# Casting weights layer by layer, and dilated attention by pairs of heads, in a four-layer decoder trunk on eight cores

## The chip, the cores and the metric

One Trainium2 chip, all eight of its cores. Each core takes two of the sixteen sequences of 4096 tokens through all four layers; the cores exchange nothing. The metric is the device time of the slowest core for one execution, in microseconds (us). Cores 0 to 3 are one die, 4 to 7 the other. Some executions are *slow*: the cores of one die, or of both, were granted a lower TensorE clock for part of the time, and the whole is some per cent longer.

Engines in the profile: PE is the TensorE matmul, PEld its weight load, DVE VectorE, ACT ScalarE, POOL GpSimd, SPq the queue on which the DMAs are issued. L763 is a line of the kernel in question.

## The reference, cut to what matters

Each layer normalises its input and projects it once (1024 to 6152 columns). It then runs two groups of heads on the result, projects their gated outputs back, and adds the input.

```python
def hybrid_layer(x, norm_g, w_in, ..., w_out):
    h = rms_norm(x, norm_g)
    proj = jnp.einsum('bsd,dn->bsn', h, w_in)            # stage A (and the gate columns, B)
    mq, mk, mv, mo, mz, mi, mf, aq, ak, av, az = jnp.split(proj, split_points, axis=-1)
    hm = mlstm_chunkwise(...)                            # stage C: 4 heads, recurrence by chunks of 64
    ...
    for window, dilation in ((128, 1), (512, 4), (2048, 16)):     # stage D: 8 heads of 64
        o, lse = dilated_window_attention(qa, ka, va, window, dilation)
    ...                                                  # outputs of the three patterns merged by lse
    y = jnp.einsum('bsm,md->bsd', jnp.concatenate([hm, ha], axis=-1), w_out)     # stage E
    return x + y
```

Attention cuts each residue class of the tokens into blocks of 128. A block of queries sees its own block of keys and the one before it. The first block of a class has no previous one. At dilation 16 a class has only 256 tokens, so every second block is a first one.

The weights come as float32 and the kernel multiplies in bfloat16, so every weight is read, scaled by norm_g where it belongs to the first projection, cast, and written back to memory once: "the weight cast".

Of the kernel before, what the change touches and what calls it, by code (L numbers as in the profile page):

```python
# [134 lines left out]
def build_program(S_TOK, NSEQ, DEPTH, debug=False):  # L135
# [24 lines left out]
    c_mask = din("c_mask", [128, 256], BF16)  # L160
# [27 lines left out]
    with ExitStack() as top:  # L188
# [14 lines left out]
        maskt = sbt(top, "maskt", [128, 256], BF16)  # L203
# [10 lines left out]

        def prologue():
            with ExitStack() as es:
                ng = sbt(es, "pl_ng", [128, DEPTH, 8], F32)
                for l in range(DEPTH):
                    S.dma('sp', ng[:, l, :], normg[l], writes=["pl_ng"])
                stg = Rot([(sbt(es, "pl_stg%d" % i, [128, 2048], F32), "pl_stg%d" % i) for i in range(3)])  # L220
                obf = Rot([(sbt(es, "pl_obf%d" % i, [128, 2048], BF16), "pl_obf%d" % i) for i in range(3)])
                engs = ['dve', 'act']
                k = 0
                for l in range(DEPTH):
                    for kc in range(8):
                        rows = slice(kc * 128, (kc + 1) * 128)
                        gcol = ng[:, l, kc:kc + 1]
                        pieces = [(w_in[l, rows, 0:2048], ws_in[l, :, kc * 6144:kc * 6144 + 2048], 2048),
                                  (w_in[l, rows, 2048:4096], ws_in[l, :, kc * 6144 + 2048:kc * 6144 + 4096], 2048),
                                  (w_in[l, rows, 4104:6152], ws_in[l, :, kc * 6144 + 4096:kc * 6144 + 6144], 2048),  # L230
                                  (w_g[l, rows, :], ws_g[l, :, kc * 256:(kc + 1) * 256], 256)]
                        for (src, dst, n) in pieces:
                            st, stk = stg.next()
                            ob, obk = obf.next()
                            S.dma('sp', st[:, 0:n], src, writes=[stk])
                            eng = engs[k % 2]
                            k += 1
                            if eng == 'act':
                                S.op('act', lambda e: e.activation(out=ob[:, 0:n], in_=st[:, 0:n], func=AF.Copy, scale=gcol),
                                     reads=[stk, "pl_ng"], writes=[obk])  # L240
                            else:
                                S.op(eng, lambda e: e.tensor_scalar(out=ob[:, 0:n], in0=st[:, 0:n], scalar1=gcol, scalar2=None, op0=ALU.mult),
                                     reads=[stk, "pl_ng"], writes=[obk])
                            S.dma('sp', dst, ob[:, 0:n], reads=[obk])
                    for mc in range(12):
                        st, stk = stg.next()
                        ob, obk = obf.next()
                        S.dma('sp', st[:, 0:1024], w_out[l, mc * 128:(mc + 1) * 128, :], writes=[stk])
                        eng = engs[k % 2]
                        k += 1  # L250
                        if eng == 'act':
                            S.op('act', lambda e: e.copy(out=ob[:, 0:1024], in_=st[:, 0:1024]), reads=[stk], writes=[obk])
                        else:
                            S.op(eng, lambda e: e.tensor_copy(out=ob[:, 0:1024], in_=st[:, 0:1024]), reads=[stk], writes=[obk])
                        S.dma('sp', ws_out[l, :, mc * 1024:(mc + 1) * 1024], ob[:, 0:1024], reads=[obk])
                S.barrier()
# [395 lines left out]
        def phase_D(l, s):  # L652
            t0 = s * S_TOK
            with ExitStack() as es:
# [5 lines left out]
                pex = Rot([(sbt(es, "D_pe%d" % i, [128, 256], BF16), "D_pe%d" % i) for i in range(4)])  # L660
                pmk = Rot([(sbt(es, "D_pm%d" % i, [128, 256], BF16), "D_pm%d" % i) for i in range(4)])
                ostg = Rot([(sbt(es, "D_os%d" % i, [128, 8, 65], F32), "D_os%d" % i) for i in range(3)])
                ps_s = Rot([(pst(es, "D_pss%d" % i, [128, 512], F32), "D_pss%d" % i) for i in range(4)])
                ps_o = Rot([(pst(es, "D_pso%d" % i, [128, 512], F32), "D_pso%d" % i) for i in range(4)])
# [32 lines left out]
                for pi, d in enumerate(PATTERNS):  # L697
# [4 lines left out]
                    for r in range(d):  # L702
                        for nb in range(nbd):
                            for h in range(8):
                                units.append((r, nb, h))
                    pending = []
                    state = {"po": None}
# [5 lines left out]
                    def emit_qk(u):  # L713
                        r, nb, h = u
                        qt, kt = QT[h // 2], KT[h // 2]
                        p0 = (h % 2) * 64
                        pss, pssk = ps_s.next()
                        W = 256 if nb > 0 else 128
                        S.op('pe', lambda e: e.matmul(pss[:, 0:128], lhsT=kt[p0:p0 + 64, tok(r, nb)], rhs=qt[p0:p0 + 64, tok(r, nb)], start=True, stop=True),  # L719
                             reads=[("KT", h // 2), ("QT", h // 2)], writes=[pssk], signal=(nb == 0))  # L720
                        if nb > 0:
                            S.op('pe', lambda e: e.matmul(pss[:, 128:256], lhsT=kt[p0:p0 + 64, tok(r, nb - 1)], rhs=qt[p0:p0 + 64, tok(r, nb)], start=True, stop=True),  # L722
                                 reads=[("KT", h // 2), ("QT", h // 2)], writes=[pssk])
                        px, pxk = pex.next()
                        S.op('act', lambda e: e.activation(out=px[:, 0:W], in_=pss[:, 0:W], func=AF.Exp, scale=0.125), reads=[pssk], writes=[pxk])  # L725
                        pm, pmk_ = pmk.next()
                        S.op('dve', lambda e: e.tensor_tensor(out=pm[:, 0:W], in0=px[:, 0:W], in1=maskt[:, 0:W], op=ALU.mult), reads=[pxk, "maskt"], writes=[pmk_])  # L727
                        pending.append((u, pm, pmk_))

                    def emit_pv():  # L730
                        (u, pm, pmk_) = pending.pop(0)
                        r, nb, h = u
                        b = r * nbd + nb
                        if h % 4 == 0:
                            state["po"] = ps_o.next()
                        po, pok = state["po"]
                        hs = (h % 4) * 65
                        S.op('pe', lambda e: e.matmul(po[:, hs:hs + 65], lhsT=pm[:, 0:128], rhs=V[:, b, h, 0:65], start=True, stop=(nb == 0)),  # L738
                             reads=[pmk_, (Vk, (b // 8) * 8), (Vk, "ones")], writes=[pok], signal=(nb == 0))
                        if nb > 0:  # L740
                            S.op('pe', lambda e: e.matmul(po[:, hs:hs + 65], lhsT=pm[:, 128:256], rhs=V[:, b - 1, h, 0:65], start=False, stop=True),  # L741
                                 reads=[pmk_, (Vk, ((b - 1) // 8) * 8), (Vk, "ones")], writes=[pok])
# [167 lines left out]
```

## The kernel before: the parts that the change touches

All engines are driven through one helper. `S.op(engine, ..., reads=[names], writes=[names])` and `S.dma('sp', out, in, reads, writes)` turn names of tiles into semaphores: an instruction waits for the last writers of what it reads, and for the last readers and writers of what it writes. `Rot([...]).next()` hands out a row of buffers in turn. There is one DMA queue, and it issues in program order.

The prologue casts all four layers ahead of everything else, one piece after the other:

```python
stg = Rot([... 3 buffers]);  obf = Rot([... 3 buffers])
for l in range(DEPTH):                       # 44 pieces a layer, 176 in all
    for (src, dst, n) in pieces:
        st, stk = stg.next();  ob, obk = obf.next()
        S.dma('sp', st[:, 0:n], src, writes=[stk])              # load
        ... cast on DVE or ACT in turn, st -> ob
        S.dma('sp', dst, ob[:, 0:n], reads=[obk])               # store: the queue waits here for the cast
```

Attention works on one head at a time. Two heads of 64 share a tile of 128 partitions: the even head is on partitions 0 to 63, the odd one on 64 to 127.

```python
ps_s = Rot([... 4 banks]);  ps_o = Rot([... 4 banks])
def emit_qk(u):
    r, nb, h = u
    p0 = (h % 2) * 64
    matmul(pss[:, 0:128],   lhsT=kt[p0:p0+64, tok(r, nb)],   rhs=qt[p0:p0+64, tok(r, nb)])      # L719, "score"
    if nb > 0:
        matmul(pss[:, 128:256], lhsT=kt[p0:p0+64, tok(r, nb-1)], rhs=qt[p0:p0+64, tok(r, nb)])  # L722, "score"
    activation(px[:, 0:W], pss[:, 0:W], Exp)                                                # ACT
    tensor_tensor(pm[:, 0:W], px[:, 0:W], maskt[:, 0:W], mult)                                # DVE
def emit_pv():                                # three units later
    matmul(po[:, hs:hs+65], lhsT=pm[:, 0:128],   rhs=V[:, b, h, 0:65])                         # L738, "value"
    if nb > 0:
        matmul(po[:, hs:hs+65], lhsT=pm[:, 128:256], rhs=V[:, b-1, h, 0:65])                   # L741, "value"
    ...  # every fourth head: copy po out on DVE or ACT; every eighth: store
for ui, u in enumerate(units):
    emit_qk(u)
    if len(pending) > 3: emit_pv()
    if ui == len(units) // 2: nextV = load_V(next dilation)     # fetch and cast the values of the next pattern
```

A score multiplies over 64 rows, a value over 128: the tensor engine changes its tiling between them, twice for each head.

## Time and profile before

20619.81 us, median of three runs (20401.18 to 20717.54).

Sums by stage, each the mean of the eight cores in the profiled execution, in us:

| stage | times | sum | each |
|---|---|---|---|
| weight cast | 1 | 1166 | |
| A projection | 8 | 7762 | 891 to 1010 |
| B gates | 8 | 647 | 81 |
| C recurrence | 8 | 2896 | 362 |
| D attention | 8 | 4463 | 557.9 |
| E output projection | 8 | 3649 | 456.1 |

The weight cast is counted from its first load, some 3.5 us after the start of the span. The spread in A goes with the clock: a projection that was granted 0.78 of full speed took some 1005 us, one that was granted 0.93 some 893. The lines of the profile stand in the prediction.

### The profile page before, as it was taken

How to read it: one execution, taken by the hardware profiler on the slowest of the kernel's cores; microseconds unless marked ns; L12 is line 12 of the kernel's file. 1: busy time of each engine (PE TensorE's matmuls, PEld its weight loads, DVE VectorE, ACT ScalarE, POOL GpSimd, SP SyncE). 2: the span in 40 equal slices, each digit the busy share in tenths (PEclk: the TensorE clock that was granted, in tenths of full speed). 3: DMA queues.
4: the chain of work that ended last, by engine and by line, in shares of the span. 5: the costliest groups of instructions: out<-in, count | busy, mean ns of one | idle time of the engine just before them, and what ended most of it. 6: DMA issues, size and time to landing. Idle time of an engine off the chain costs nothing.

```text
span 20716.2 us, 272538 instructions; the slowest of 8 cores (20382.5 to 20716.2 us)
## 1 busy us (share of the span) xinstructions
PE 13746.5 (66%) x64640; PEld 6212.6 (30%) x64640; DVE 7589.5 (37%) x17544; ACT 7610.3 (37%) x17513; POOL 1010.3 (5%) x1084
## 2 busy tenths in 40 slices
PE   0059376883869657695667928597476965779376
PEld 0023232332323223232323314233232322334232
DVE  0023542335423353234432354233542345323542
ACT  0034351434514353243513435143542435324451
POOL 0000000000000000000000000000000000000000
PEclk9997556875578656776568755787557765678657
DMA  4431225313242233423233131522324223332324
GB/s 166 166 129 70 98 87 151 105 69 122 85 161 75 81 108 111 138 73 97 92 136 114 71 118 69 179 78 71 118 96 150 77 83 106 117 132 75 100 88 151
DMA packets 1331733, 2233.47 MB, mean 108 GB/s; under 512 B 108304, under 2 KB 739344, under 8 KB 1306640
## 3 DMA queue, kind: packets, MB, share of 16 engines
q1 hardware_dynamic: 1330192, 2216.04, 31.3%
q8 instruction: 587, 9.62, 0.2%
q14 instruction: 954, 7.82, 0.1%
HBM read 1308.49 MB, written 907.15 MB: 107 GB/s over the span
## 4 chain that ended last, share of the span: by engine, by line
PE 58%; ACT 11%; DMA 10%; DVE 10%; issue 6%; SPq 2%; POOL 2%; DVEq 0%; ACTq 0%; POOLq 0%
PE A_pm_u L337 19%; PE E_py_u L827 9%; PE A_pm_u L330 9%; PE D_pss_u L719 7%; PE D_pso_u L738 5%; DMA D_Vstg_u<-s_av 3%; PE D_pss_u L722 3%; DMA pl_stg_u<-w_in 3%; ACT C_sqj_u L643 3%; SPq L108 2%; DVE C_t_u L639 1%; POOL E_ga_u L811 1%; ACT C_kw_u L609 1%; ACT A_sqj_u L300 1%; PE C_pso_u L623 1%
## 5 line engine op out<-in xcount | busy, mean ns | idle before, releaser
L337 PE MATMUL A_pm_u<-A_Wb_u,A_hT_u 128*128 128x512 bf16 x16384 | 4262.4, 425 | 0.0
L725 ACT ACTIVATE D_pe_u<-D_pss_u 128x256 bf16<-128x256 f32 (+1 forms) x6144 | 2200.1, 362 | 1228.4 <-ACT D_pe_u L725 455.9
L337 PEld LDWEIGHTS A_pm_u<-A_Wb_u,A_hT_u 128*128 128x128 bf16 x16384 | 1746.6, 107 | 2388.4 <-issue 1990.7
L727 DVE TENSOR_TENSOR D_pm_u<-D_pe_u,maskt_u 128x256 bf16<-128x256 bf16 (+1 forms) x6144 | 1692.8, 277 | 1911.5 <-PE D_pso_u L741 771.4
L330 PE MATMUL A_pm_u<-A_hT_u,A_Wb_u 128*128 128x512 bf16 x8192 | 2347.3, 440 | 0.0
L719 PE MATMUL D_pss_u<-D_Q_u,D_K_u 64*128 64x128 bf16 x6144 | 2044.9, 335 | 220.2 <-DMA D_K_u<-s_akT 218.8
L827 PE MATMUL E_py_u<-E_Wo_u,E_gT_u 128*128 128x512 bf16 x6144 | 1887.8, 479 | 174.4 <-DVE E_gT_u L822 174.4
L738 PE MATMUL D_pso_u<-D_V_u,D_pm_u 128*128 128x65 bf16 x6144 | 1450.2, 236 | 732.8 <-DVE D_pm_u L727 730.9
L722 PE MATMUL D_pss_u<-D_Q_u,D_K_u 64*128 64x128 bf16 x4800 | 1560.1, 325 | 0.0
L817 ACT COPY E_gT_u<-E_ptr_u 128x1024 bf16<-128x1024 bf16 x256 | 259.2, 1013 | 3291.4 <-PE E_ptr_u L815 3272.1
L738 PEld LDWEIGHTS D_pso_u<-D_V_u,D_pm_u 128*128 128x128 bf16 x6144 | 645.4, 105 | 2121.7 <-issue 2092.7
L330 PEld LDWEIGHTS A_pm_u<-A_hT_u,A_Wb_u 128*128 128x128 bf16 x8192 | 894.5, 110 | 1200.1 <-issue 1003.4
L358 DVE SCALAR_TENSOR_TENSOR A_acc_u<-A_cbuf_u,A_cw_u,A_acc_u 128x512 f32<-128x512 f32 x1536 | 1153.9, 751 | 164.5 <-DVE A_acc_u L358 3.2
L315 PE MATMUL A_ptr_u<-identb_u,A_xn_u 128*128 128x128 bf16 x2048 | 204.4, 260 | 1508.6 <-DMA A_xt_u<-x 1201.1
L741 PE MATMUL D_pso_u<-D_V_u,D_pm_u 128*128 128x65 bf16 x4800 | 1165.1, 243 | 0.0
L827 PEld LDWEIGHTS E_py_u<-E_Wo_u,E_gT_u 128*128 128x128 bf16 x6144 | 700.9, 117 | 1300.9 <-issue 957.4
L623 PE MATMUL C_pso_u<-C_Cb_u,C_q_u 128*128 128x257 bf16 x1024 | 420.2, 410 | 972.5 <-ACT C_Cb_u L612 972.5
L829 DVE TENSOR_TENSOR E_xo_u<-E_xt_u,E_py_u 128x512 f32<-128x512 f32 x512 | 352.1, 688 | 1778.5 <-PE E_py_u L827 1772.0
L621 PE MATMUL C_pso_u<-C_v_u,C_ST_u 128*128 128x257 bf16 x1024 | 411.9, 402 | 826.6 <-DVE C_ST_u L605 733.3
L643 ACT ACTIVATE C_sqj_u<-C_t_u 128x256 bf16<-128x256 f32 x1024 | 427.2, 417 | 1414.6 <-DVE C_t_u L639 1332.5
L355 DVE TENSOR_SCALAR A_acc_u<-A_cbuf_u,A_cw_u 128x512 f32<-128x512 f32 x512 | 249.2, 487 | 1884.8 <-ACT A_cbuf_u L354 1884.8
L719 PEld LDWEIGHTS D_pss_u<-D_Q_u,D_K_u 64*128 64x128 bf16 x6144 | 715.4, 117 | 744.3 <-issue 225.6
(98 smaller groups left out, 14543.5 us busy)
## 6 DMA issues: line engine op xcount, KB each, us to landing
s_od<-D_os_u SPq DMA_DIRECT2D x768, 260.0 KB, 2.1
E_o_u<-s_od SPq DMA_DIRECT2D x256, 780.0 KB, 6.9
pl_stg_u<-w_in SPq DMA_DIRECT2D x96, 1024.0 KB, 5.5
A_Wb_u<-ws_in SPq DMA_DIRECT2D x96, 1024.0 KB, 12.7
xs<-E_xo_u SPq DMA_DIRECT2D x192, 512.0 KB, 3.0
A_xt_u<-xs SPq DMA_DIRECT2D x192, 512.0 KB, 5.4
E_xt_u<-xs SPq DMA_DIRECT2D x192, 512.0 KB, 5.0
s_o<-A_tmo_u SPq DMA_DIRECT2D x256, 256.0 KB, 2.0
```

The source lines that it names most:

```text
L330: S.op('pe', lambda e: e.matmul(ps[:], lhsT=wtile[:, kc, col0:col0 + 128], rhs=hTt[:, kc, :], start=(kc == 0), stop=(kc == 7)), reads=[hk] ...
L337: S.op('pe', lambda e: e.matmul(ps[:], lhsT=hTt[:, kc, j * 128:(j + 1) * 128], rhs=Wb[:, kc, col0:col0 + 512], start=(kc == 0), stop=(kc = ...
L358: S.op('dve', lambda e: e.scalar_tensor_tensor(out=a[:], in0=cbuf[:, c, jt:jt + 512], scalar=cw[:, c, jt:jt + 1], in1=a[:], op0=ALU.mult, ...
L623: S.op('pe', lambda e: e.matmul(ps_o[:, h, 0:257], lhsT=q[:, h, ts], rhs=Cb[:, h, 0:257], start=False, stop=True), reads=[qk_, ("Cb", h)], ...
L643: S.op('act', lambda e: e.activation(out=sqj[:], in_=t1[:, h, :], func=AF.Square, accum_out=smt[:, 8 + h:9 + h]), reads=[(t1k, h)], writes ...
L719: S.op('pe', lambda e: e.matmul(pss[:, 0:128], lhsT=kt[p0:p0 + 64, tok(r, nb)], rhs=qt[p0:p0 + 64, tok(r, nb)], start=True, stop=True), re ...
L722: S.op('pe', lambda e: e.matmul(pss[:, 128:256], lhsT=kt[p0:p0 + 64, tok(r, nb - 1)], rhs=qt[p0:p0 + 64, tok(r, nb)], start=True, stop=Tru ...
L725: S.op('act', lambda e: e.activation(out=px[:, 0:W], in_=pss[:, 0:W], func=AF.Exp, scale=0.125), reads=[pssk], writes=[pxk])
L727: S.op('dve', lambda e: e.tensor_tensor(out=pm[:, 0:W], in0=px[:, 0:W], in1=maskt[:, 0:W], op=ALU.mult), reads=[pxk, "maskt"], writes=[pmk_])
L738: S.op('pe', lambda e: e.matmul(po[:, hs:hs + 65], lhsT=pm[:, 0:128], rhs=V[:, b, h, 0:65], start=True, stop=(nb == 0)), reads=[pmk_, (Vk, ...
L741: S.op('pe', lambda e: e.matmul(po[:, hs:hs + 65], lhsT=pm[:, 128:256], rhs=V[:, b - 1, h, 0:65], start=False, stop=True), reads=[pmk_, (V ...
L827: S.op('pe', lambda e: e.matmul(pyt[:], lhsT=gTt[:, mc, :], rhs=Wo[:, mc, half * 512:(half + 1) * 512], start=(mc == 0), stop=(mc == 11)), ...
```

## The change

Its intent is threefold. (1) Only layer 0's weights are cast in the prologue, with six staging and four output buffers, and five loads in flight: load k+5 is issued ahead of store k. (2) The 132 pieces of layers 1 to 3 are loaded, cast (on ACT) and stored in the output projection of the layer before, one for each 128-token tile, 22 in each of the first six of those stages. (3) Attention works on pairs of heads: the score matmuls alternate between the two row halves and write to two PSUM banks; one exponential and one mask multiplication serve both heads; then come the pair's values.

```diff
 prologue:
-for l in range(DEPTH): ... load; cast; store
+cst = Caster(es, 0, "pl")              # 6 staging buffers, 4 output buffers
+pcs = weight_pieces(0)
+lds = [cst.load(p) for p in pcs[:5]]
+for k in range(len(pcs)):
+    c = cst.cast(lds.pop(0), 'dve' if k % 2 == 0 else 'act')
+    if k + 5 < len(pcs):
+        lds.append(cst.load(pcs[k + 5]))
+    cst.store(c)

 phase_D:
-ps_s: 4 x [128, 512]     ps_o: 4 x [128, 512]
+ps_s: 3 x [128, 2, 512]  ps_o: 2 x [128, 512]    mask4 = maskt[:, 256:768]
 def emit_qk(u):
-    r, nb, h = u ... two matmuls of one head
+    r, nb, p = u
+    for w in range(nw):                       # own block, previous block
+        for a in range(2):                    # even head, odd head
+            ro = slice(a * 64, a * 64 + 64)
+            matmul(pss[:, a, w*128:(w+1)*128], lhsT=KT[p][ro, tok(r, nb - w)], rhs=QT[p][ro, tok(r, nb)])
+    activation(px[:, 0:W] as (a, w, i), pss[:, :, 0:128*nw], Exp)        # 512 columns
+    tensor_tensor(pm[:, 0:W], px[:, 0:W], mask4[:, 0:W], mult)
 def emit_pv():
+    for a in range(2):  ... the one or two value matmuls of head 2p + a
     ...

 phase_E, for each tile:
+    after the first transposes' copy:  if loaded: casted.append(cst.cast(loaded.pop(0)))      # ACT
+    after the tile's output store:     if casted: cst.store(casted.pop(0))
+                                       if jobs:   loaded.append(cst.load(jobs.pop(0)))
```

(Cut: the class `Caster`, the order of the pieces, the wider mask constant, and the split of the output staging's name in two.)

## The prediction

> **What bounds the kernel now.** I read in this order: the table of cores, the page, busy times by stage, then the timeline inside the stages that the change edits. The profiled run counts as slow (20717.54 us, 1.6% above the fastest of three at 20401.18), so I take the stages' inner structure from it and not its absolute level.
>
> The page:
>
> ```profile
> PE 13746.5 (66%) x64640; PEld 6212.6 (30%) x64640; DVE 7589.5 (37%) x17544; ACT 7610.3 (37%) x17513; POOL 1010.3 (5%) x1084
> PEclk9997556875578656776568755787557765678657
> ```
>
> Matmul time leads but there is no engine at its limit over the whole span; the clock row moves between 0.5 and 0.9, so the program is a row of stages with different limits. Busy times by stage (core 5: window and length, then PE, weight load, DVE, ACT, POOL, then clock, DMA share, GB/s). The lines are: weight cast, then projection, gates, recurrence, attention, output projection of the first sequence, then three stretches inside attention.
>
> ```profile
> 0.00:1181.27 1181.27, 0.00 (x0) 0.00 (x0) 98.95 (x88) 106.74 (x89) 0.20 (x4) 1.00 0.48 165
> 1181.27:2158.07 976.80, 861.10 (x3520) 365.36 (x3520) 299.83 (x432) 411.27 (x695) 80.38 (x97) 0.84 0.25 88
> 2158.07:2243.16 85.09, 6.59 (x32) 6.14 (x32) 34.84 (x16) 12.37 (x5) 0.10 (x1) 0.51 0.13 51
> 2243.16:2608.12 364.96, 118.51 (x640) 76.26 (x640) 227.35 (x640) 165.64 (x576) 7.91 (x3) 0.56 0.36 116
> 2608.12:3170.79 562.67, 447.96 (x2736) 209.20 (x2736) 245.78 (x870) 315.95 (x870) 1.04 (x2) 0.50 0.24 84
> 3170.79:3624.33 453.54, 269.07 (x1152) 116.12 (x1152) 128.27 (x224) 32.41 (x32) 36.85 (x32) 0.73 0.56 166
> 2614.00:2641.00 27.00, 0.58 (x4) 0.27 (x4) 1.23 (x1) 0.00 (x0) 0.00 (x0) 0.50 0.96 341
> 2726.00:2742.00 16.00, 0.00 (x0) 0.00 (x0) 2.45 (x2) 5.71 (x2) 0.00 (x0) 0.50 0.65 213
> 2886.00:2923.00 37.00, 0.00 (x0) 0.00 (x0) 2.45 (x2) 6.79 (x2) 0.00 (x0) 0.50 0.34 103
> ```
>
> The first 1181 us hold no matmul, and DMA is only half used: a serial chain. The five stages after it come eight times (four layers, two sequences); attention costs about 558 us each time, 4466 in all. In attention PE is busy 80% at half clock, apart from three stretches of 27, 16 and 37 us in which everything waits for loads.
>
> Why the weight cast is serial (timeline; start, length, what):
>
> ```profile
> 506.19 0.38 SPq L108 DMA_DIRECT2D pl_stg_u<-w_in  x1
> 511.45 1.29 DVE L242 TENSOR_SCALAR pl_obf_u<-pl_stg_u,pl_ng_u 128x2048 bf16<-128x2048 f32 x1 [10.68 <-DMA pl_stg_u<-w_in]
> 512.87 0.33 SPq L108 DMA_DIRECT2D ws_in<-pl_obf_u  x1
> 513.29 0.38 SPq L108 DMA_DIRECT2D pl_stg_u<-w_in  x1
> ```
>
> The next load is issued only after the previous piece's store, because the one queue waits for the cast before that store: one load in flight, though there are three buffers. 513.29 - 506.19 = 7.1 us for a 1 MB piece.
>
> What sets attention's pace (timeline, PE): a full head of dilation 1 or 4, the start of the next, then a full head of dilation 16 and, last, two lone first matmuls of the whole stage.
>
> ```profile
> 2930.35 0.29 PE L719 MATMUL D_pss_u<-D_Q_u,D_K_u 64*128 64x128 bf16 x1
> 2930.46 0.29 PE L722 MATMUL D_pss_u<-D_Q_u,D_K_u 64*128 64x128 bf16 x1
> 2930.68 0.24 PE L738 MATMUL D_pso_u<-D_V_u,D_pm_u 128*128 128x65 bf16 x1
> 2930.73 0.24 PE L741 MATMUL D_pso_u<-D_V_u,D_pm_u 128*128 128x65 bf16 x1
> 2930.91 0.29 PE L719 MATMUL D_pss_u<-D_Q_u,D_K_u 64*128 64x128 bf16 x1
> ```
> ```profile
> 2997.43 0.43 PE L719 MATMUL D_pss_u<-D_Q_u,D_K_u 64*128 64x128 bf16 x1
> 2997.68 0.41 PE L722 MATMUL D_pss_u<-D_Q_u,D_K_u 64*128 64x128 bf16 x1
> 2998.02 0.24 PE L738 MATMUL D_pso_u<-D_V_u,D_pm_u 128*128 128x65 bf16 x1
> 2998.19 0.43 PE L719 MATMUL D_pss_u<-D_Q_u,D_K_u 64*128 64x128 bf16 x1
> ```
> ```profile
> 2617.91 0.29 PE L719 MATMUL D_pss_u<-D_Q_u,D_K_u 64*128 64x128 bf16 x2 [24.96 <-DMA D_K_u<-s_akT]
> ```
>
> Score to score takes 0.11 us, score to value 0.22, value to value 0.05, back to score 0.17: 0.55 us a head, repeated without a wait. The two crossings between 64-row and 128-row matmuls are the dear steps. At dilation 16 the steps are 0.25, 0.34 and 0.17 (0.76; the second value matmul's record is missing). The last line is the key: those two scores are heads 0 and 1, on different halves of the rows. Together they take 0.29 us, the length of one; in sequence they would take 0.40. They ran at once.
>
> **What the Trainium skill says.** "TensorEngine Tiling (Array Packing)", Key Properties: tiles can load weights and multiply in parallel, but changing the tiling mode drains the array. "TensorE: Matmul & The Clock Gate", Part 3, puts the starts of matmuls on different row groups about 4 ns apart. The trace agrees with both: 0.29 us for two, and 0.22 and 0.17 us at the crossings against 0.11 and 0.05 without. Its Part 1 says that the clock is halved until the array has been busy for a window: attention stands at 0.50 throughout. "DMA: Bandwidth & Descriptors", Specifications, limits HBM to about 358 GB/s a core; the first attention stretch above shows 341.
>
> **The change part by part.**
>
> *Weight cast ahead of layer 0.* It casts 44 pieces in place of 176, with five loads in flight. Bytes: 24 pieces of 1.05 MB, 8 of 0.13, 12 of 0.52 are 32.5 MB read and 16.3 written, 48.8 MB. At 341 GB/s that is 143 us; add some 15 for the first load and the last cast and store: 158. Casts take half of what 176 do (about 100 us each on DVE and ACT, so 25 each now) and hide. Saved: 1181 - 158 = about 1020 us.
>
> *The other 132 pieces, in the output projection of layers 0 to 2*, 22 to each of six stages of 32 tiles. ACT does the cast; it is busy 32 of 454 us there, 2.0 us a piece fits. A tile has taken 13.7 us (two tiles' stores are issued at 3404.29 and 3417.95), set by a chain PE, DVE, POOL, PE, DVE, PE. DMA moves 166 GB/s x 13.7 = 2.3 MB per tile; a large piece adds 1.57 MB, 3.85 MB in all, 11.3 us at 341 GB/s. It fits, barely: the piece's store and load are issued ahead of the loads of the tile after next, so the attention outputs arrive 4 to 5 us later, and they had 4.8 us of slack (issued at 3406.06, 6.9 us to landing by the page of DMA issues, needed at 3417.8). I allow 0.5 us for the 72 large pieces: +40 us.
>
> *Attention by pairs of heads.* The same matmuls, but scores of both heads of a pair alternate between row halves and PSUM banks, and one crossing each way serves two heads. Dilations 1 and 4: 0.11 (two steps of simultaneous scores) + 0.22 + 3 x 0.05 + 0.17 = 0.65 us a pair, before 2 x 0.55 = 1.10. First blocks, with no previous keys: 0.22 + 0.05 + 0.17 = 0.44 for 2 x 0.39. Dilation 16: 0.25 + 0.34 + 0.15 + 0.17 = 0.91 for 1.52; first blocks (half of them) 0.37 + 0.05 + 0.17 = 0.59 for 1.07. Per stage, 236 + 20 pairs at dilations 1 and 4 and 64 + 64 at dilation 16:
> before 236 x 1.10 + 20 x 0.78 + 64 x 1.52 + 64 x 1.07 = 441 us; after 236 x 0.65 + 20 x 0.44 + 64 x 0.91 + 64 x 0.59 = 258. Saved 183, eight times 1464. The loads' stretches (80 us) and the ends (30) stay. The exponential drops from two of 385 ns to one: 256 columns cost 385, 128 cost 279, so 512 about 597, plus a quarter of a 372 ns copy, 0.69 us by durations. That is just above 0.65, but ACT overlaps its own instructions: four 128-column exponentials take 0.77 us at 2654.52, a step of 0.16. DVE: 224 and 291 ns give 425 + 106 = 0.53. So PE still sets the pace, closely; I take 65 us off for it. Saved: 1400.
>
> *Sum.* -1020 + 40 - 1400 = -2380. From 20,620 (median) that is 18,240; from the fast level, near 20,510 (the mean of the two lower runs), 18,130. I say 18,200.
>
> **The rivals.**
> 1. The pairs do not run at once in the steady stream (the weight loads or a bank stand in the way). Then two more 0.11 (0.25 at dilation 16) steps: 0.87 and 1.41 us, saving about 100 us a stage, 800 in all; 18,800. Against it: the two first scores. For it: only isolated scores show it; four consecutive ones at 2992.13 took 0.73 us, which is more than two steps but much less than four of 0.25.
> 2. The clock wakes. I summed the columns streamed in each clock window of the trace: half-clock windows that were followed by a higher clock were streaming for 0.69 to 0.78 of their time at least, attention for (0.21 + 0.11)/0.55 = 0.58. A pair gives (0.21 + 0.22)/0.65 = 0.66: just short. If it wakes, ACT sets 0.55 to 0.6 us a pair: 100 to 200 us less, 18,000.
> 3. The output projection becomes DMA-bound with large pieces: 15.5 us a tile, 72 x 1.8 = 130 us; 18,300.
> 4. ACT or the two output banks (four before) become attention's wait: 0.75 us a pair, 24 us a stage, 190 us; 18,400.
> 5. Less idle time heats the chip and the projection's clock (0.84 here) drops: 1% of 7,900 us. Small.
>
> **Range and chances.** The weight cast is nearly sure (±40). Attention carries the width: 800 to 1650. With the output projection and the spread of 1.5% between states: 17,850 to 18,650. Even the worst rivals together leave about 8% gained: faster 0.98, within 2% 0.015, slower 0.005.
>
> **What would show it.** First projection's start near 160 us, DMA share above 0.9 before it. Attention stages of about 380 us, a full pair's period of 0.65 us, both scores of a pair within 0.01 us of each other, clock still 0.50; ACT busy around 90% of the steady stretches. Output projection 460 to 475 us in layers 0 to 2, 454 in layer 3. Projection and recurrence unchanged. I am wrong if the attention stage exceeds 430 us (no overlap, or a new wait on ACT), if it drops below 350 (clock awake), or if large pieces make tiles of 15 us.

## The result, and the profile after

18287.71 us, median of 13 runs (17629.31 to 18528.76), against 20589.26 for the kernel before (16 runs). The ratio of fast runs is 0.8784, 95% interval 0.8647 to 0.8921. The record's own class for this comparison is "unclear"; only two of the changed kernel's executions were fast. The interval lies wholly under 0.98 and the changed kernel's slowest run (18528.76) is below the old one's fastest (20003.31). A ratio here is the mean time of one kernel's fast runs over that of the other's in the same rounds, so it isn't quite the ratio of the medians. Taking each kernel's fastest dies, called undisturbed here (mean granted clock 0.739 before, 0.743 after), the medians of the die are 19,955 to 19,977 us before and 17,527 to 17,541 after: about 2,430 us less, again a ratio of 0.878.

By stage, mean of eight cores, in us:

| stage | before | after | difference | predicted |
|---|---|---|---|---|
| weight cast | 1166 | 158 | -1008 | -1020 |
| A projection | 7762 | 7664 | -98 (clock state) | 0 |
| B, C | 3543 | 3537 | -6 | 0 |
| D attention | 4463 | 3042 | -1421 | -1400 |
| E output projection | 3649 | 3676 | +27 | +40 |

Busy times by stage of the slowest core (window and length, then PE, weight load, DVE, ACT, POOL with counts, then clock, DMA share, GB/s): weight cast, projection, attention and output projection of the first sequence, and last a steady stretch of attention.

```profile
0.00:163.06 163.06, 0.00 (x0) 0.00 (x0) 17.28 (x22) 39.60 (x23) 0.20 (x4) 1.00 0.91 301
163.06:1173.59 1010.53, 899.69 (x3520) 374.89 (x3520) 299.84 (x432) 411.78 (x695) 80.39 (x98) 0.80 0.24 85
...
1619.90:2002.70 382.80, 264.95 (x2736) 141.21 (x2736) 185.03 (x486) 249.41 (x486) 1.04 (x2) 0.50 0.35 123
2002.70:2472.39 469.69, 279.41 (x1152) 119.02 (x1152) 129.19 (x224) 67.52 (x54) 36.84 (x32) 0.69 0.66 216
1860.00:1880.00 20.00, 19.66 (x232) 11.31 (x231) 14.52 (x39) 18.50 (x39) 0.00 (x0) 0.50 0.30 109
```

The weight cast now keeps the DMA at 0.91 of its time where it had been at 0.48. Attention has the same 2736 matmuls, but they cover 265 us where they covered 448, because two of them are under way at a time and the busy time of an engine counts a moment once. In the steady stretch PE is busy 98% and ACT 93%: the two are nearly level. The output projection carries 22 more ACT instructions (54 for 32) and its DMA share goes from 0.56 to 0.66.

The page's busy row and its clock row show the same from farther away:

```profile
PE 12315.5 (67%) x64640; PEld 5674.8 (31%) x64640; DVE 7025.5 (38%) x14406; ACT 7200.7 (39%) x14507; POOL 1010.4 (6%) x1084
...
PEclk8865677756777567775677756777567875689657
...
L766 ACT ACTIVATE D_pe_u<-D_pss_u 128x512 bf16<-128x512 f32 (+1 forms) x3072 | 1673.0, 554 | 309.8 <-PE D_pss_u L763 98.0
```

No matmul was removed (64640 in both), and the attention scores' mean length hardly changed (331 ns; 335 and 325 for the two lines before); PE's busy time fell by 1431 us through overlap. At the left of the clock row, three slices of 0.9, in which hardly anything was multiplied, have become one of 0.8. The last line is the new exponential: 554 ns on average over full and first blocks.

The prologue (timeline: start, length, what):

```profile
79.58 0.59 SPq L108 DMA_DIRECT2D pl_s_u<-w_in  x1
82.92 1.29 DVE L276 TENSOR_SCALAR pl_o_u<-pl_s_u,pl_ng_u 128x2048 bf16<-128x2048 f32 x1 [10.78 <-DMA ws_in<-pl_o_u]
84.35 0.33 SPq L108 DMA_DIRECT2D ws_in<-pl_o_u  x1
84.83 0.56 SPq L108 DMA_DIRECT2D pl_s_u<-w_g  x1
87.09 0.63 SPq L108 DMA_DIRECT2D pl_s_u<-w_in  x1
```

The load at 79.58 is issued *ahead* of the cast at 82.92 and its store at 84.35, and it is the load of the fifth piece after that one. The cast had waited for an output buffer to be stored (`<-DMA ws_in<-pl_o_u`), not for its load: at this place the chain no longer waits for a load, and the DMA is 0.91 busy.

A full pair of heads at dilation 4 and the start of the next (PE timeline), then one at dilation 16:

```profile
1781.72 0.40 PE L763 MATMUL D_pss_u<-D_Q_u,D_K_u 64*128 64x128 bf16 x4
1782.06 0.23 PE L784 MATMUL D_pso_u<-D_V_u,D_pm_u 128*128 128x65 bf16 x1
1782.10 0.25 PE L787 MATMUL D_pso_u<-D_V_u,D_pm_u 128*128 128x65 bf16 x1
1782.15 0.25 PE L784 MATMUL D_pso_u<-D_V_u,D_pm_u 128*128 128x65 bf16 x1
1782.21 0.24 PE L787 MATMUL D_pso_u<-D_V_u,D_pm_u 128*128 128x65 bf16 x1
1782.39 0.41 PE L763 MATMUL D_pss_u<-D_Q_u,D_K_u 64*128 64x128 bf16 x4
```
```profile
1940.48 0.67 PE L763 MATMUL D_pss_u<-D_Q_u,D_K_u 64*128 64x128 bf16 x4
1941.08 0.29 PE L784 MATMUL D_pso_u<-D_V_u,D_pm_u 128*128 128x65 bf16 x2
1941.31 0.67 PE L763 MATMUL D_pss_u<-D_Q_u,D_K_u 64*128 64x128 bf16 x4
```

From 1781.72 to 1782.39 is 0.67 us for a pair, where two heads had taken 2 x 0.55. Four scores cover 0.40 us, no more than two in sequence had. The raw starts of those four show why (us):

```
1781.720  1781.724   1781.825  1781.828
```

Two and two, 3 to 4 ns apart within a couple, 0.10 between the couples. At dilation 16 a class has four pairs of a first block and then four of a full one, and values follow their scores three pairs later. So three of four full pairs (four scores) go beside two values, as here, and three of four first pairs (two scores) beside four values; only the fourth of each goes beside values of its own kind.

### The profile page after: what moved, and what is told of

Read it like the earlier page. It is cut to its first block, busy times and chain, and to the rows that moved or that the text cites.

```text
span 18286.3 us, 242923 instructions; the slowest of 8 cores (17814.7 to 18286.3 us)
## 1 busy us (share of the span) xinstructions
PE 12315.5 (67%) x64640; PEld 5674.8 (31%) x64640; DVE 7025.5 (38%) x14406; ACT 7200.7 (39%) x14507; POOL 1010.4 (6%) x1084
## 4 chain that ended last, share of the span: by engine, by line
PE 59%; ACT 11%; DVE 10%; DMA 8%; issue 7%; SPq 3%; POOL 2%; DVEq 0%; ACTq 0%; POOLq 0%
PE A_pm_u L377 21%; PE A_pm_u L370 10%; PE E_py_u L883 10%; PE D_pss_u L763 6%; PE D_pso_u L784 4%; DMA D_Vstg_u<-s_av 3%; ACT C_sqj_u L683 3%; SPq L108 2%; DVE C_t_u L679 2%; POOL E_ga_u L865 2%; ACT C_kw_u L649 2%; PE C_pso_u L663 1%; ACT A_sqj_u L340 1%; PE D_pso_u L787 1%; PE C_psc_u L666 1%
## 5 line engine op out<-in xcount | busy, mean ns | idle before, releaser
L763 PE MATMUL D_pss_u<-D_Q_u,D_K_u 64*128 64x128 bf16 x10944 | 1354.9, 331 | 944.8 <-ACT D_pe_u L766 690.7
L766 ACT ACTIVATE D_pe_u<-D_pss_u 128x512 bf16<-128x512 f32 (+1 forms) x3072 | 1673.0, 554 | 309.8 <-PE D_pss_u L763 98.0
L770 DVE TENSOR_TENSOR D_pm_u<-D_pe_u,maskt_u 128x512 bf16<-128x512 bf16 (+1 forms) x3072 | 1206.0, 395 | 954.4 <-ACT D_pe_u L766 317.3
L784 PE MATMUL D_pso_u<-D_V_u,D_pm_u 128*128 128x65 bf16 x6144 | 1013.8, 238 | 47.9 <-DVE D_os_u L795 20.3
L402 ACT ACTIVATE A_fmo_u<-A_acc_u,A_cb_u 128x512 bf16<-128x512 f32 x512 | 370.1, 723 | 1489.1 <-DVE A_acc_u L398 1488.3
L876 PE MATMUL E_pt_u<-identb_u,E_ga_u 128*128 128x128 bf16 x1024 | 142.2, 288 | 1183.9 <-POOL E_ga_u L865 1183.9
L763 PEld LDWEIGHTS D_pss_u<-D_Q_u,D_K_u 64*128 64x128 bf16 x10944 | 461.8, 123 | 1236.0 <-issue 959.5
L787 PE MATMUL D_pso_u<-D_V_u,D_pm_u 128*128 128x65 bf16 x4800 | 844.2, 244 | 0.0
L421 DVE SCALAR_TENSOR_TENSOR A_fmo_u<-A_pm_u,A_qg_u,A_rs_u 128x512 bf16<-128x512 f32 x512 | 384.3, 751 | 1139.2 <-ACT A_rs_u L418 976.0
```

Source lines behind the costliest of these rows:

```text
L763: S.op('pe', lambda e: e.matmul(pss[:, a, w * 128:(w + 1) * 128], lhsT=KT[p][ro, tok(r, nb - w)], rhs=QT[p][ro, tok(r, nb)], start=True, s ...
L766: S.op('act', lambda e: e.activation(out=px[:, 0:W].rearrange("p (w a i) -> p a w i", a=2, i=128), in_=pss[:, :, 0:128 * nw].rearrange("p ...
L770: S.op('dve', lambda e: e.tensor_tensor(out=pm[:, 0:W], in0=px[:, 0:W], in1=mask4[:, 0:W], op=ALU.mult), reads=[pxk, "maskt"], writes=[pmk_])
L784: S.op('pe', lambda e: e.matmul(po[:, hs:hs + 65], lhsT=pm[:, a * 128:(a + 1) * 128], rhs=V[:, b, h, 0:65], start=True, stop=(nb == 0)), r ...
L787: S.op('pe', lambda e: e.matmul(po[:, hs:hs + 65], lhsT=pm[:, 256 + a * 128:256 + (a + 1) * 128], rhs=V[:, b - 1, h, 0:65], start=False, s ...
```

## The experiments

Twelve kernels ran on the chip; each is an edit of the changed kernel. All gave the reference's result but e3. In attention "a pair" is a full pair at dilations 1 and 4 in the steady stream, and "stage" the mean attention stage over eight cores: 557.9 us before, 380.2 after.

### Does the gain come from scores running at once? e3_same_half

Both heads of a pair read the even head's rows. Same counts, banks and instructions, but no two different row halves (a wrong result).

```diff
-ro = slice(a * 64, a * 64 + 64)
+ro = slice(0, 64)
```

> Both heads of a pair take keys and queries of rows 0 to 63, so their scores cannot run at once (the result is wrong on purpose); crossings stay one each way for a pair, and ACT and DVE do just the same. Theory (half the attention gain is overlap of the two row halves): scores start 0.11 us apart, a full pair of dilation 1 or 4 takes 0.67 + 0.22 = 0.88 us, of dilation 16 about 1.42; the attention stage 380 + 100 = 480 us, the whole about 19,000. Rival (the gain is fewer and wider ACT and DVE instructions): stage stays at 380 to 390.

Measured: pair 0.873 to 0.902 us, stage 473.9. (19057.61 us in all, median of three runs, all slow; the stage has its usual clock of 0.50.) The attention stage of the slowest core, and one pair in the PE timeline:

```profile
1591.04:2068.39 477.35, 363.37 (x2736) 213.72 (x2736) 191.00 (x486) 257.87 (x486) 1.04 (x2) 0.50 0.28 99
```
```profile
1789.97 0.64 PE L763 MATMUL D_pss_u<-D_Q_u,D_K_u 64*128 64x128 bf16 x4
1790.54 0.23 PE L784 MATMUL D_pso_u<-D_V_u,D_pm_u 128*128 128x65 bf16 x1
...
1790.70 0.24 PE L787 MATMUL D_pso_u<-D_V_u,D_pm_u 128*128 128x65 bf16 x1
1790.87 0.64 PE L763 MATMUL D_pss_u<-D_Q_u,D_K_u 64*128 64x128 bf16 x4
```

Four scores now take 0.64 us instead of 0.40; their raw starts are 1789.972, 1790.077, 1790.196 and 1790.316, steps of 0.11 to 0.12. The values' steps didn't move. So different row halves are worth 94 us a stage (473.9 - 380.2), and the first rival of the prediction falls. It also shows that nearly half of the gain is something else.

### Is it one crossing for two heads? e6_interleave

The pair's instructions stay, but the scores of the even head are followed by the values of an older even head, then the odd ones. The tiling changes four times a pair, as before, and scores of different halves no longer meet.

```diff
-emit_qk(u);  if len(pending) > LAG: emit_pv()
+qk_half(c, 0)
+if old: pv_half(old, 0)
+qk_half(c, 1);  exp_mask(c)
+if old: pv_half(old, 1)
```

> PE order scores of head 0, values of head 0 of an older pair, scores of head 1, values of head 1: four crossings between 64-row and 128-row matmuls for a pair, as before the change, and no overlap of halves; exponential and mask stay paired. Result right. Theory: 2 x 0.55 = 1.10 us a pair at dilations 1 and 4, 1.52 at 16; stage 545 to 560 us, the whole gain of attention gone; e6 minus e3 (about 75 us) is what the shared crossings are worth. Rival (paired ACT and DVE instructions made the gain): stage below 420.

Measured: pair 1.093 to 1.107 us, stage 555.8; 19068.17 us in all.

```profile
1512.77:2070.08 557.31, 445.33 (x2736) 208.47 (x2736) 191.69 (x486) 257.56 (x486) 1.04 (x2) 0.50 0.24 85
```
```profile
1650.23 0.39 PE L759 MATMUL D_pss_u<-D_Q_u,D_K_u 64*128 64x128 bf16 x2
1650.55 0.24 PE L786 MATMUL D_pso_u<-D_V_u,D_pm_u 128*128 128x65 bf16 x1
1650.60 0.24 PE L789 MATMUL D_pso_u<-D_V_u,D_pm_u 128*128 128x65 bf16 x1
1650.78 0.39 PE L759 MATMUL D_pss_u<-D_Q_u,D_K_u 64*128 64x128 bf16 x2
...
1651.32 0.39 PE L759 MATMUL D_pss_u<-D_Q_u,D_K_u 64*128 64x128 bf16 x2
```

Score to value is 0.32 from the first of two scores, value back to score 0.18: the old pattern, and the old time (557.9). ACT is as lightly loaded as in the change (257.56 us, 486 instructions), and it helps nothing. With e3 the gain splits cleanly: shared crossings 555.8 - 473.9 = 82 us, overlap 473.9 - 380.2 = 94; together 176 of the 177.7 measured.

### Is it the fewer, larger instructions on ACT and DVE? e5_split_exp

Two exponentials and two masks of 256 columns a pair, as before the change; PE's order as after it.

```diff
-activation(px, pss[:, :, 0:128*nw], Exp);  tensor_tensor(pm, px, mask4, mult)
+for a in range(2):
+    activation(px[a], pss[:, a, 0:128*nw], Exp);  tensor_tensor(pm[a], px[a], mask4[a], mult)
```

> Exponential and mask are split again, one for each head of the pair (256 columns, as before the change); matmul order as in the changed kernel. Result right. Theory (PE sets the pace, ACT close behind at 0.55 to 0.6 us a pair): stage 380 to 400 us, at most a little more as ACT has less room. Rival (the gain is fewer ACT and DVE instructions): two exponentials and their waits take as long as before, about 0.55 each, stage 500 or more.

Measured: stage 381.2; 18172.15 us in all.

```profile
1621.00:2006.81 385.81, 264.84 (x2736) 141.64 (x2736) 214.68 (x870) 264.99 (x870) 1.04 (x2) 0.50 0.36 123
```

870 instructions on ACT in place of 486 cost 15.6 us more of its busy time (264.99 against 249.41) and 1 us of the stage. Merging them isn't where the time came from, though ACT's and DVE's busy times went down in the change and look like a cause.

### Does the order of the four scores matter? e4_head_order

```diff
-for w in range(nw):
-    for a in range(2):
+for a in range(2):
+    for w in range(nw):
```

> Same matmuls, order head by head (head 0 current, head 0 previous, head 1 current, head 1 previous) in place of alternating. Result right. Theory: starts stay in program order, so only the middle two can overlap; a full pair takes one score step more, 0.67 + 0.105 = 0.77 us (dilation 16: 0.91 + 0.25), first blocks unchanged; stage 380 + 24 + 16 = 420 us. Rival (the array sorts it out by itself, any order of independent halves is as good): 380.

Measured: stage 382.8, pair 0.667 to 0.673; 17962.36 us in all (median of two; the fast one 17604.74). **A miss**: I expected the program order even, even, odd, odd to let only the middle two meet, 420 us a stage.

```profile
1510.62:1896.74 386.12, 266.13 (x2736) 142.07 (x2736) 185.10 (x486) 249.37 (x486) 1.04 (x2) 0.50 0.36 122
```
```profile
1680.47 0.40 PE L763 MATMUL D_pss_u<-D_Q_u,D_K_u 64*128 64x128 bf16 x4
...
1681.14 0.41 PE L763 MATMUL D_pss_u<-D_Q_u,D_K_u 64*128 64x128 bf16 x4
```

Raw starts of the four (us):

```
1680.469  1680.475   1680.574  1680.579
```

Two start 6 ns apart, then two more a tenth later. Scores on one half are 0.11 apart at least (e3), so the two that start together can't be the first two of the program, which are on one half: the third must have gone ahead of the second. That is inferred: the trace's records don't name the rows, and they don't show whether the order was changed on the chip or before it, when the program was compiled. What is shown is that the order inside the group of four doesn't matter. Only what stands between scores does (e6).

### Are the parts independent? e1_attn_only and e2_cast_only

The first has the changed attention with the old prologue and no casting in the output projection; the second the changed casts with the old attention.

```diff
 e1:  prologue() as before; in phase_E no jobs; phase_D as after
 e2:  prologue() and phase_E as after; phase_D as before
```

> The kernel before with the attention part of the change alone (weight cast as before, nothing cast in the output projection). Theory: attention stages fall from 557 to 380 us as in the full change, eight times 177 = 1420 us less, ratio to before 0.93; weight cast 1165 to 1180 us, output projection 454. Rival (the parts need each other, for instance attention gains because the clock or the memory is quieter after a short weight cast): stage clearly off 380.

> The weight-cast part alone, attention as before. Theory: first projection starts near 160 us, 1020 less; output projections of layers 0 to 2 take 2 to 10 us more each (15 to 50 in all); attention 557; ratio to before 0.952. With the attention part alone at 0.93 the two add up to 0.88. Rival (the projection pays for it in clock, as there is no cold start): ratio 0.97 or more.

Measured: e1 18632.11 us in its fast run (19337.55 the median, with slow runs), e2 19140.6. Weight cast and first attention stage of e1, then weight cast, attention and output projection of e2:

```profile
0.00:1190.40 1190.40, 0.00 (x0) 0.00 (x0) 98.97 (x88) 106.63 (x89) 0.20 (x4) 1.00 0.49 164
2594.27:2975.03 380.76, 265.29 (x2736) 141.60 (x2736) 185.46 (x486) 248.96 (x486) 1.04 (x2) 0.50 0.35 124
```
```profile
0.00:163.80 163.80, 0.00 (x0) 0.00 (x0) 17.28 (x22) 39.57 (x23) 0.20 (x4) 1.00 0.93 300
1510.21:2071.80 561.59, 448.15 (x2736) 210.11 (x2736) 246.22 (x870) 315.71 (x870) 1.04 (x2) 0.50 0.24 84
2073.07:2530.00 456.93, 265.77 (x1130) 116.14 (x1152) 128.31 (x224) 67.46 (x54) 36.89 (x32) 0.74 0.63 221
```

Each part makes the same gain alone as together: attention 381.7 in e1 (380.2), weight cast 158 in e2 (158), E 3656 in e2 against 3649 before. Undisturbed dies stand at 18,570 us (e1) and 18,980 (e2), so 1,390 and 980 less than the 19,960 of before; the two sum to 2,370 of the 2,430.

### Which half of the cast's gain is which? e9_all_ahead and e10_one_in_flight

e9 casts all 176 pieces in the prologue, but with five loads in flight. e10 casts only layer 0 there, with the six and four buffers of the change, but issues each load after the previous store.

```diff
 e9
-pcs = weight_pieces(0)
+pcs = [piece for l in range(DEPTH) for piece in weight_pieces(l)]      # and no jobs in phase_E
 e10
-lds = [cst.load(p) for p in pcs[:5]]
+lds = [cst.load(p) for p in pcs[:1]]
     c = cst.cast(lds.pop(0), ...)
-    if k + 5 < len(pcs): lds.append(cst.load(pcs[k + 5]))
     cst.store(c)
+    if k + 1 < len(pcs): lds.append(cst.load(pcs[k + 1]))
```

> Changed kernel, but the weights of all four layers are cast ahead, with five loads in flight; the output projection casts nothing. Theory: 4 x 143 us of transfer + 15 = 587 us before the first projection, output projections all 454 (in the changed kernel 456 to 467 in layers 0 to 2): 400 us longer than the changed kernel. So of the 1020 us saved, some 590 come from keeping loads in flight and 430 from moving three layers' cast under the output projection. Rival (pipelining is everything, or nothing): 160 to 250, or 1100.

> Changed kernel, but in the cast ahead of layer 0 the next load is issued after the store of the piece before it, as before the change; six and four buffers stay. Theory (the queue's order made it serial, not the number of buffers): 44 x 6.7 = 295 us before the first projection in place of 158. Rival (the buffers made the gain): 160 to 200.

Measured, mean of the cores: weight cast 613 us in e9, 297 in e10; in all 18833.36 and 18074.36 us. The weight cast of each, e9 first:

```profile
0.00:615.90 615.90, 0.00 (x0) 0.00 (x0) 69.12 (x88) 154.44 (x89) 0.20 (x4) 1.00 0.97 317
```
```profile
0.00:300.30 300.30, 0.00 (x0) 0.00 (x0) 17.28 (x22) 39.57 (x23) 0.20 (x4) 1.00 0.49 164
```

In e10 the DMA is back at 0.49 and 164 GB/s, the rate of before, with all the buffers in place: the place of a load in the queue's order made the chain, and more buffers alone don't end it. Whether fewer buffers would have done with the new order, no run shows. By e9, of the 1008 us saved, 553 (1166 - 613) are from keeping loads in flight and 455 (613 - 158) from moving three layers under the output projection, at a price of up to 25 us there (E 3676 in the change's profile, 3651 in e9; other runs of the change's casts lie between).

### Why didn't the clock rise? e11_wake

Two matmuls of 256 columns with all 128 rows, whose result nobody reads, are put ahead of the scores of the first 32 pairs of each dilation.

```diff
+state["n"] = state.get("n", 0) + 1
+if state["n"] <= 32:
+    for a in range(2):
+        matmul(pss[:, a, 256:512], lhsT=identb[:], rhs=maskt[:, 0:256])
```

> Changed kernel with two 128-row matmuls of 256 columns put ahead of the scores of the first 32 pairs of each dilation (their output is overwritten or unused, result right). These pairs then stream for (0.43 + 0.43)/1.09 = 0.79 of the time at half clock. Theory (the clock follows the time in which the array streams, and two row halves at once count once, so that 0.66 is not enough): granted clock above 0.5 within 10 us of each dilation's start, and it stays up only if an awake pair (0.22 us of streaming in about 0.6) is enough. If it stays: pairs of 0.58 to 0.6 us, set by ACT, stage near 350. If it falls back: stage 385 to 400. Rival (something else holds attention at 0.5): clock 0.5 throughout, stage 380 + 3 x 32 x 0.43 = 420.

Measured: stage 402.8; 18541.55 us in all, three slow runs. First attention stage of the slowest core: with the dummies, after them (dilation 1), then the same at dilation 4.

```profile
1678.00:1697.00 19.00, 17.94 (x276) 9.66 (x274) 13.73 (x36) 17.55 (x36) 0.00 (x0) 1.00 0.27 101
1700.00:1780.00 80.00, 58.65 (x702) 32.91 (x700) 44.94 (x112) 62.50 (x112) 0.00 (x0) 0.50 0.37 127
1791.00:1810.00 19.00, 18.72 (x242) 9.51 (x240) 12.12 (x33) 15.88 (x34) 0.00 (x0) 1.00 0.24 87
1812.00:1850.00 38.00, 18.34 (x216) 10.64 (x214) 14.10 (x35) 16.02 (x33) 0.00 (x0) 0.50 0.34 113
```

The clock rose while the dummies ran (20.5 us each time here, 20.5 to 27.3 over all cores and stages; at dilation 16 never, which the expectation had wrong) and fell back soon after they stopped, though the ordinary stream of pairs went on: the last dummy started at 1692.87, the clock fell at 1697.8, and in between no two matmuls started more than 0.92 us apart. I expected 385 to 400 if it fell back; it was 402.8, so I had set the dummies' cost a little low. I added up the columns streamed in each clock window of 3.4 us. In the changed kernel, attention's half-clock windows reach 0.94 to 1.04 of a window if every matmul's columns count in full, yet only 0.63 to 0.68 if a 64-row matmul counts half. In e11 the windows before the two rises have 0.97 and 1.02 by the first count, which is nothing special, but 0.78 and 0.83 by the second. The second count also orders the other stages. Taken a little finer, by the time that each matmul streamed inside the window, it gives this for the slowest cores of the old kernel, the changed one and e11: where the clock rose after a half-clock window, that window had at least 0.72, and no window above 0.78 was followed by half clock again; attention without dummies never passed 0.66. (The short gate stage, with rises after 0.41 to 0.50, doesn't fit.) So the pairs fall short of what wakes the clock. Whether two halves at once count once, or a 64-row matmul counts half wherever it runs, no run separates.

A second thing stands in the first line: at full clock with dummies ACT was busy 17.55 of 19 us. By my estimate ACT needs about 0.61 us a pair (17.55 us over some 29 pairs, four fifths of its 36 instructions), so a full clock alone would leave little to win.

### What is left in attention? e7_v_early, e8_v_early_spread, e12_v_pieces

In the change three stretches of each stage still wait for loads: 80 us by the prediction. One, at the start, is for the stage's own first queries, keys and values (the longest gap there is 24 us in the first stage of the changed kernel); the other two are for the next pattern's values (22 and 41 us). e7 fetches those at the start of the pattern before, into four staging buffers, and casts them where they were cast; e8 also spreads the casts (all on DVE, 12 pairs apart); e12 adds to e8 a finer name for each part of a staging buffer.

```diff
 e7
-Vstg: 2 buffers;   at half of the pattern: nextV = load_V(next)              # fetch and cast
+Vstg: 4 buffers;   at its start: fetched = fetch_V(next);  at half: cast_V, all four
 e8
+if ui >= len(units) // 2 and ui % 12 == 0 and fetched[2]: cast_V(fetched, all_dve=True)
 e12
-S.dma('sp', vs[:, o_:o_ + nbd_, :], srcv[r_], writes=[vsk])
+S.dma('sp', vs[:, o_:o_ + nbd_, :], srcv[r_], writes=[(vsk, o_ // 2)])          # the cast reads all four
```

> Changed kernel with four staging buffers for the values in place of two, and the values of the next dilation fetched at the start of the present one; their casts stay where they were (half way, DVE and ACT in turn). Result right. Theory (the standstills inside attention are waits for those fetches, unchanged by the change: 17 and 38 us): they shrink to the casts, 5 to 8 us each; stage 380 to 335-345 us, 300 us in all, ratio to before about 0.865. Rival (the fetch is not the wait, or the early fetch delays the stores): stage 370 or more.

> As the run before, but the four casts are all on DVE and twelve pairs apart. Result right. Theory: a 1.2 us cast on DVE, which is busy 0.5 of a pair's 0.67 us, is made good within a few pairs; stage 325 to 335 us, 400 us less than the changed kernel, ratio to before about 0.86. Rival (DVE becomes the bound around the casts): as e7 or above.

Measured: stages 359.8 and 352.0, where I had expected 335 to 345 and 325 to 335. In all 18035.61 us (6 runs) and 17896.59 us (8 runs), medians with mostly slow runs; on undisturbed dies some 17,370 and 17,300. **Both partly missed**: the gain is there, but a wait remained. The waits of e8 around the start of dilation 16's fetch (engine, line, tile, what it waited for, total, times, longest), then its DMA queue:

```profile
PE D_pso_u L794 <- DVE D_os_u L805: 31.8, 5, 30.6
...
DVE D_os_u L805 <- DMA s_od<-D_os_u: 30.6, 1, 30.6
ACT D_os_u L807 <- DMA s_od<-D_os_u: 29.9, 1, 29.9
```
```profile
4030.39 34.31 SPq L108 DMA_DIRECT2D D_Vstg_u<-s_av  x15
4064.90 10.23 SPq L108 DMA_DIRECT2D s_od<-D_os_u  x6
```

At dilation 16 a staging buffer is filled by four small fetches, all booked under one name. A writer waits for the last writer of its name, so the queue waits for each to land before issuing the next: the 15 issues shown take 34 us, 2.3 us each. Output stores stand behind them in the same queue, output buffers stay full, the copies wait for the stores, and PE waits for the copies. The first line alone would have blamed DVE; the two under it name the DMA, and only the queue's own timeline shows that the stores hadn't been issued at all.

> The run before last (early fetch, casts spread on DVE) with one edit: the four pieces of a staging buffer at dilation 16 are booked under four names in place of one, so that the queue issues them one behind the other without waiting for each to land. Result right. Theory (of the 38 us standstill before dilation 16, some 31 us are the queue waiting 16 times 2.7 us for pieces that don't overlap, and in the two early-fetch runs this only moved, to stores that could not be issued): stage 352 to 318-328 us, 220 us less in all than e8; no gap above 10 us between exponentials after the start. Rival (the small pieces need that time in the memory): stage stays at 350.

Measured: stage 327.8, at the upper edge of what was expected. The sixteen fetches for dilation 16 are now issued in 9.6 us:

```profile
1721.38 9.57 SPq L108 DMA_DIRECT2D D_Vstg_u<-s_av  x16
```

After the start no gap in the stage is longer than 6.4 us; the wait for the stage's own first loads is still there (its longest gap 28 us in this stage). In all 17639.81 us (17254.81 to 17922.03, 7 runs; fast ones 17254.81 and 17482.81) beside 20524.86 for the kernel before. Its first attention stage:

```profile
1579.87:1916.42 336.55, 265.38 (x2736) 141.62 (x2736) 188.36 (x490) 235.29 (x482) 1.04 (x2) 0.50 0.41 140
```

PE's busy time is that of the change (265); 46 us of waiting are gone. On undisturbed dies it stands at 17,097 to 17,115 us against 17,527 to 17,541 for the change: about 430 us less, and the eight stages account for 8 x (380.2 - 327.8) = 419. This version beats both kernels.

## Why the prediction was right, point by point

The prediction said 18,200 us, in a range of 17,850 to 18,650; measured was 18,288. It was right for its own reasons, with one misreading; that attention's number came so near is in part luck, because errors of some 60 us went both ways.

- **Weight cast.** 158 us predicted, 158 measured, by bytes over DMA throughput. The throughput was 301 GB/s with start and end included, where the sum took 341 and added 15 us for the ends. Saved were 1008 for 1020, since the old cast was 1166 in the mean of the cores and from its first load, and not 1181 as on the slowest core from the start of the span. That the queue's order made the chain is shown by e10.
- **Output projection.** +40 predicted, +27 in the change's profile, and -2 to +18 in other runs of the same code (e12, e4, e3, e2 and others). Over-allowed: the late attention outputs that it was for didn't show. DMA-bound tiles (rival 3) didn't show: 460.7 us a stage in layers 0 to 2, at a DMA share of 0.66.
- **Attention, the steps.** Predicted 0.65 us a pair, measured 0.660 to 0.667 in the steady stream: 0.10 between couples of scores, 0.23 score to value, 0.05 between values, 0.18 back. The lone pair of scores in the old trace, two in 0.29 us, was a true sign of what the steady stream does. e3 and e6 confirm both terms, overlap and shared crossings, each by itself. Rival 1 fell by e3: its 0.87 is what came out when I took the halves away.
- **Attention, dilation 16.** Predicted 0.91 us for a full pair and 0.59 for a first one; measured 0.83 and 0.69 for three of four, where the values beside the scores are of the other kind, and 0.935 and 0.585 for the fourth, where they are of the same. In the mean a full and a first pair make 1.52 together, for 1.50 predicted. Not seeing this mixture is the **misreading**: the prediction says of dilation 16 that "the second value matmul's record is missing". It wasn't missing; the value at that place was that of a head without previous keys, which has one. For the new kernel the sum over full and first blocks hid it, as the two come in equal number. For the old one it did not: a full head took 0.80 us in the mean and not 0.76, a first one 0.55, so that dilation 16 cost some 173 us a stage where the prediction summed 166.
- **Attention, the discount.** The model gave 1464 us and I took off 65 for ACT; measured 1421. So 43 us were due, and they are a net of larger errors. Over the eight stages of the slowest core a full pair at dilations 1 and 4 took 0.684 us in the mean, since one in fifteen is held up and takes 0.72 us or more: 8 us a stage beyond the 0.65 of the sum, some 64 in all. Against that the old stage's dilation 16 was dearer than the sum by those 7 us a stage, some 56 in all. (The remaining 35 us are spread over the new dilation 16 and the first blocks; I haven't worked them out.) That the held-up pairs wait for ACT isn't shown. Part of them wait for the output banks, two where there had been four: in the first attention stage after its start PE waits for the copy that frees one (total, times, longest), a wait that the old kernel's dilation 1 and 4 didn't have:

```profile
PE D_pso_u L784 <- DVE D_os_u L795: 2.9, 10, 0.3
```

  So rival 4 (two output banks, or ACT, as a new wait) came about only in small, 0.684 us a pair and not 0.75. ACT is near, with 93% in the steady stretch beside PE's 98%; e5 shows that splitting its instructions changes the stage by 1 us.
- **Clock.** It stayed at 0.50, as said, and "just short" is borne out: 0.63 to 0.68 of a window against the 0.78 and 0.83 after which it rose (e11). By the estimate of 0.61 us for ACT, rival 2 would also have paid less than I gave it.
- **Rival 5**, heat, can't be told from the clock's own states: the sum of A is 98 us lower in the change's profile and varies by over 100 us a stage in both kernels.

What I left unexamined in the prediction were the 80 us of loads' stretches, which I took as given. Some 50 us of them a stage went with three small edits, 419 us in all (e12).

## What to carry to other kernels

Read the steps from one matmul to the next rather than their lengths: the dear ones here were changes between 64-row and 128-row work, and grouping what has the same tiling, with the two row halves side by side, was worth a third of the stage without one instruction less on PE. In a single in-order queue, buffers don't make a pipeline: a load has to be issued ahead of the store that waits, and small transfers booked under one name wait for each other and hold up everything behind them. When a wait names an engine, follow it one step further, to the queue's own timeline.

## What the Trainium skill lacked or had wrong

- "TensorE: Matmul & The Clock Gate", Part 3, "What overlaps and what doesn't", says that matmuls keep strict program order in start and end. In e4, with both scores of one head ahead of the other's, the starts were 1680.469, 1680.475, 1680.574 and 1680.579, though two scores on one half need 0.11 us (e3). Either the third started ahead of the second, or the program's order was changed before it reached the chip, which no trace here shows; the page's rule would have cost 37 us a stage (420 expected, 382.8 measured). The 4 ns between row groups that the same part gives was right: 3 to 6 ns.
- The same page, Part 1, doesn't say what share of a window has to be busy. Here, with a 64-row matmul counted half, 0.63 to 0.68 of a window stayed at 0.50, and 0.78 and 0.83 were followed by 1.0; by finer counting the clock rose after 0.72 at least (the gate stage aside). Its return to the lower clock "after ≥1 idle window" is too narrow: in e11 the clock fell 4.9 us after the last dummy, with no pause of over 0.92 us between starts of matmuls; the window before the fall was streaming for about half of its time.
- "TensorEngine Tiling (Array Packing)", Key Properties, says that a change of mode drains the array and gives no figure. At half clock the step into 128-row work took 0.22 us and back 0.17, against 0.11 and 0.05 without a change; sharing them was worth 82 us a stage (e6 against e3).
- "SBUF — State Buffer", Door 1, gives lines of 16 bytes and bfloat16 steps of up to 8 elements as free. The traces agree as far as they go: scores follow each other at 0.11 us at dilations 1 and 4 and at 0.25 at dilation 16. The page has no figure for TensorE's operands beyond that step, and no run here separates the weights' read from the moving operand's.
